# Linear attention on one core: the first half of Q is loaded by GpSimd with a cast instead of by SP in f32

## The chip, the core and the metric

The kernel runs on one core of one Trainium2 chip. The metric is the device time of one execution in microseconds (us). The median of three runs of the kernel before is 126.54 us (126.53 to 126.78).

## The reference

```python
def setup_inputs():
    batch, heads, seq, dim = 8, 12, 512, 64      # Q, K, V: f32, [8, 12, 512, 64] each
...
    Q_feat = np.maximum(0, Q) + 1
    K_feat = np.maximum(0, K) + 1
    KV = np.einsum('bhkd,bhkv->bhdv', K_feat, V)
    K_sum = np.sum(K_feat, axis=2)
    numerator = np.einsum('bhqd,bhdv->bhqv', Q_feat, KV)
    denominator = np.einsum('bhqd,bhd->bhq', Q_feat, K_sum)
    return (numerator / (denominator[:, :, :, None] + 1e-10)).astype(np.float32)
```

There are 96 heads of 512 rows by 64. Three inputs of 12.58 MB each are read and one output of 12.58 MB is written, all f32 in DRAM.

## The kernel before

The 96 heads are worked on in twelve groups of eight heads (`NG` is 12), and two groups share one input buffer and one output buffer. K, V and Q are loaded into SBUF as bf16: the DMA that GpSimd issues reads f32 from DRAM and casts on its way (`load`, `load_q`). Only the first half of the first Q buffer is different: SP issues a DMA of f32 into a tile of its own, `q_first` (L93), since the DMAs that SP issues here move data as it is. The other half of that buffer, `u[:, 1]` of `q_raw`, is loaded by GpSimd with the cast (L98).

For each group VectorE makes the features of K and Q (`feature`, L146: add 1, then max with 1), VectorE and ScalarE lay V out in blocks (`v_blocks`, L162 and L164), TensorE multiplies K's features with V (`keys_values`, L180) and transposes Q's features (L201), TensorE makes the output (L214), and VectorE divides (`norms`, L231 and L232). GpSimd issues the stores of the first ten groups (L135); SP issues the last three store DMAs (L138 and L141).

The order of all instructions is written out by hand under `tc.manual_schedule()`: each engine runs its instructions in the order of the program text and waits only for the data that it needs. So the order of the lines at L257 to L273 is the order in which GpSimd issues the first loads and does its memsets. It is:

```python
        nc.gpsimd.memset(zero, 0.0)
        q_first = load_first_q()
        load("k", (0,))
        load("v", (0,))
        load_rest_q(q_first)
        load("k", (1,))
        load("v", (1,))
```

After these GpSimd builds `identity` for the transposes and clears the sixteen parts of `kva_all` (L271), and then it issues the loads of the next pair (`load_pair(1)`). `zero` is a [128, 1] tile of f32 zeros. ScalarE copies it, broadcast, into parts of `v_all` (L250), and VectorE clears the rest of `v_all` (L249). The input pool has two buffers of each kind, so the load of a later pair waits until VectorE and ScalarE have read the buffer that it overwrites.

Of the kernel before, what the change touches and what calls it, by code (L numbers as in the profile page):

```python
# [8 lines left out]
FP32 = mybir.dt.float32  # L9
BF16 = mybir.dt.bfloat16  # L10
# [9 lines left out]
def kernel(  # L20
# [19 lines left out]
    nc = tc.nc  # L40

    B, H, S, D = Q.shape
    P = 128
    C = 8
    C2 = 2 * C
    C4 = 4 * C
# [7 lines left out]
    def view(t, c):  # L54
        return t.flatten_outer_dims().rearrange("(n p c) d -> p n c d", p=P, c=c)

    q_eights = view(Q, C4)
# [2 lines left out]
    o_dram = view(out, C)  # L60

    const = ctx.enter_context(tc.tile_pool(name="const", bufs=1))
    head_pool = ctx.enter_context(tc.tile_pool(name="head_pool", bufs=1))
    in_pool = ctx.enter_context(tc.tile_pool(name="in_pool", bufs=IN_BUFS))
    kf_pool = ctx.enter_context(tc.tile_pool(name="kf_pool", bufs=2))
    qf_pool = ctx.enter_context(tc.tile_pool(name="qf_pool", bufs=3))
# [11 lines left out]
    zero = const.tile([P, 1], FP32, name="zero")  # L78
# [4 lines left out]
    raw = {}  # L83
    bufs = {}
# [3 lines left out]
    outs = {}  # L88
    cells_of = {}

    def load_first_q():
        t = head_pool.tile([P, C4, D], FP32, name="q_first")
        nc.sync.dma_start(out=t, in_=q_eights[:, 0])  # L93
        return t

    def load_rest_q(t):
        u = in_pool.tile([P, 2, C4, D], BF16, name="q_raw")
        nc.gpsimd.dma_start(out=u[:, 1], in_=q_eights[:, 1])  # L98
        for e in range(2):
            raw["q", e] = [  # L100
                x.rearrange("p (r c) d -> p r c d", c=C)[:, :, 4 * e : 4 * e + 4]
                for x in (t, u[:, 1])
            ]

    def load(x, groups):
        s = groups[0] // 2
        if groups[0] % 2 == 0 or (x, s) not in bufs:
            bufs[x, s] = in_pool.tile([P, 4, C2, D], BF16, name=f"{x}_raw")
        if len(groups) == 2:
            ms = slice(0, 4)  # L110
            of = slice(4 * s, 4 * s + 4)
        else:
            ms = slice(groups[0] % 2, 4, 2)
            of = slice(4 * s + groups[0] % 2, 4 * s + 4, 2)
        nc.gpsimd.dma_start(out=bufs[x, s][:, ms], in_=drams[x][:, of])  # L115
        for g in groups:
            raw[x, g] = bufs[x, s][:, g % 2 : 4 : 2]
# [8 lines left out]
    def load_pair(s):  # L126
        load("k", (2 * s, 2 * s + 1))
        load("v", (2 * s, 2 * s + 1))
        load_q(s)

    def store(g):
        s = g // 2
        o_to = o_dram[:, 2 * NP * s : 2 * NP * s + 2 * NP]
        if g < NG - 2:
            nc.gpsimd.dma_start(out=o_to[:, g % 2 : 2 * NP : 2], in_=outs[s][:, g % 2 : 2 * NP : 2])  # L135
            return
        if g == NG - 2:
            nc.sync.dma_start(out=o_to[:, 0 : 2 * NP : 2], in_=outs[s][:, 0 : 2 * NP : 2])  # L138
            return
        for h in range(2):  # L140
            nc.sync.dma_start(  # L141
                out=o_to[:, 2 * h + g % 2 : 2 * NP : NP], in_=outs[s][:, 2 * h + g % 2 : 2 * NP : NP]
            )
# [6 lines left out]
    def k_features(g):  # L150
        k_raw = raw.pop(("k", g))
        kf = kf_pool.tile([P, C2, 2, D], BF16, name="kf")
        for n in range(2):
            feature(kf[:, :, n], k_raw[:, n])
        kfs[g] = kf

    def v_blocks(g):
        v_raw = raw.pop(("v", g))
        for b in range(4):
            ps = slice(32 * b, 32 * b + 32)  # L160
            if b == 3:
                nc.scalar.copy(out=v_all[ps, g % 2, :, :, b * D : b * D + D], in_=v_raw[ps])  # L162
            else:
                nc.vector.tensor_copy(  # L164
                    out=v_all[ps, g % 2, :, :, b * D : b * D + D], in_=v_raw[ps]
                )

    def q_features(g):
        q_raw = raw.pop(("q", g))
        qf = qf_pool.tile([P, R, C // 2, 2, D], BF16, name="qf")  # L170
        for n in range(2):
            feature(qf[:, :, :, n], q_raw[n])
        qfs[g] = qf

    def keys_values(g):
        kf = kfs.pop(g)
        kva_ps = psum_kva.tile([P, 4 * D1], FP32, name="kva_ps")
        for c in range(C2):
            for n in range(2):
                nc.tensor.matmul(  # L180
                    kva_ps[64 * n : 64 * n + 64],
                    lhsT=kf[:, c, n, :],
                    rhs=v_all[:, g % 2, n, c, :],
                    start=(c == 0),
                    stop=(c == C2 - 1),
                )
        kva = kva_diag[g % NV]
        for n in range(2):
            ps = slice(64 * n, 64 * n + 64)
            nc.scalar.copy(out=kva[ps, :, n, 0:D], in_=kva_ps[ps, 0 : 4 * D].rearrange("p (b d) -> p b d", b=4))  # L190
            nc.scalar.copy(out=kva[ps, :, n, D], in_=kva_ps[ps, 4 * D : 4 * D1])  # L191

    def transposes(g):
        qf = qfs.pop(g)
        if g % 2 == 0:
            qts[g // 2] = mid_pool.tile([P, C, P, R], BF16, name="qt")
        for half in range(2):
            qt_ps = psum_qt.tile([P, 2, R, P], BF16, name="qt_ps")
            for c in range(2):
                for r in range(R):  # L200
                    nc.tensor.transpose(qt_ps[:, c, r], qf[:, r, 2 * half + c, :, :], identity)  # L201
            copy = nc.vector.tensor_copy if half and g == NG - 2 else nc.scalar.copy
            lo = g % 2 * 4 + 2 * half
            copy(out=qts[g // 2][:, lo : lo + 2], in_=qt_ps.rearrange("p c r q -> p c q r"))  # L204
# [36 lines left out]
    def output(g):  # L241
        for h in range(2):
            out_matmuls(g, h)
            norms(g, h)

    def clear(i):
        t = v_all[:, i].rearrange("p n c x -> p (n c x)").bitcast(FP32)
        w = t.shape[1] * 5 // 8
        nc.vector.memset(t[:, 0:w], 0.0)  # L249
        nc.scalar.copy(out=t[:, w:], in_=zero.to_broadcast([P, t.shape[1] - w]))  # L250
        nc.vector.tensor_copy(
            out=v_all[:, i, :, :, 4 * D : 4 * D1].rearrange("p n c j -> p (n c) j"),
            in_=ones[:, None, :].to_broadcast([P, 2 * C2, 4]),
        )

    with tc.manual_schedule():
        nc.gpsimd.memset(zero, 0.0)  # L257
        q_first = load_first_q()
        load("k", (0,))
        load("v", (0,))  # L260
        load_rest_q(q_first)
        load("k", (1,))
        load("v", (1,))
        nc.vector.memset(ones, 0.0)
        for b in range(4):
            nc.vector.memset(ones[32 * b : 32 * b + 32, b : b + 1], 1.0)
        clear(0)
        make_identity(nc, identity)
        for t in kva_diag:
            for b in range(4):  # L270
                nc.gpsimd.memset(t[:, b], 0.0)  # L271
        load_pair(1)
        clear(1)  # L273
        last = NG - 1
        for g in range(last - 1):
            if g % 2:
                transposes(g - 1)
            k_features(g)
            v_blocks(g)
            if g >= 2:  # L280
                output(g - 2)
            if g % 2:
                transposes(g)
            else:
                q_features(g)
                q_features(g + 1)
            keys_values(g)
            if g % 2 and g // 2 + 2 < NG // 2:
                load_pair(g // 2 + 2)
            if g >= LAG:  # L290
                store(g - LAG)
        k_features(last - 1)
        output(last - 3)
        out_matmuls(last - 2, 0)
        v_blocks(last - 1)
        k_features(last)
        v_blocks(last)
        keys_values(last - 1)
        store(last - 1 - LAG)
        q_features(last - 1)  # L300
        q_features(last)
        norms(last - 2, 0)
        transposes(last - 1)
        out_matmuls(last - 2, 1)
        norms(last - 2, 1)
        transposes(last)
        keys_values(last)
        output(last - 1)
        output(last)
        for g in range(last - LAG, NG):  # L310
            store(g)
# [30 lines left out]
```

## Time and profile before

| | us |
|---|---|
| median of three runs | 126.54 |
| the profiled execution | 126.47 |
| its span, first to last instruction | 124.7 |
| VectorE (DVE) busy | 90.1 |
| TensorE (PE) busy | 64.2 |
| ScalarE (ACT) busy | 59.6 |
| GpSimd (POOL) busy | 26.1 |

The profiled execution took 1.8 us more than its span; that part lies around the instructions. In the profile "DMA" is the mean busy share of the core's sixteen DMA engines and "GB/s" is what they moved, counted by the bytes written: a load with the cast reads two bytes from DRAM for each byte that it writes into SBUF. Queue q0 (software_dynamic) carries the DMAs that GpSimd issues; q1 (hardware_dynamic) carries those that SP issues. A line "POOL ... DMA_DIRECT2D" is the time in which GpSimd makes the descriptors of a DMA, not the time in which its data moves.

### The profile page before, as it was taken

Reading aid. Unit: us, or ns where it says so; the run is one execution under the profiler, and the core shown is the slowest. Engines: PE = TensorE matmul, PEld = TensorE weight load, DVE = VectorE, ACT = ScalarE, POOL = GpSimd, SP = SyncE. Lnnn points to the kernel's source line nnn. Section 1 sums busy time; section 2 is a strip of 40 time slices with the busy share of each in tenths; the row PEclk is TensorE's granted clock in tenths of the full one; section 3 lists DMA queues with packets and bytes.
Section 4 is the critical chain, followed back from the end, with each engine's and each line's share of the span. In section 5 each row is a group of like instructions: output and inputs, shape, how many; then the busy total and the mean of one; then the engine's idle time right before and its main releaser. Section 6 shows DMA issues by size and latency. Waiting matters only on the chain.

```text
span 124.7 us, 2349 instructions
## 1 busy us (share of the span) xinstructions
PE 64.2 (52%) x960; PEld 52.6 (42%) x960; DVE 90.1 (72%) x190; ACT 59.6 (48%) x86; POOL 26.1 (21%) x53
## 2 busy tenths in 40 slices
PE   0000874600596837939099690069394369874200
PEld 0000654600475826829088490058183158663000
DVE  4875735206999989998999950799958799969700
ACT  7505169806009981398803981603982283650000
POOL 6992020400001460207202070302020200020000
PEclk9999999995559996799855999657999855999655
DMA  3999999999999999999999999999999999999993
GB/s 89 320 212 216 206 211 212 212 215 218 206 212 212 220 213 206 212 215 217 230 406 327 210 212 219 212 342 395 230 202 215 219 247 417 419 417 415 406 409 135
DMA packets 11819, 32.13 MB, mean 258 GB/s; under 512 B 544, under 2 KB 544, under 8 KB 11680
## 3 DMA queue, kind: packets, MB, share of 16 engines
q0 software_dynamic: 10592, 28.84, 97.5%
q1 hardware_dynamic: 1216, 3.15, 6.7%
q8 instruction: 7, 0.11, 0.3%
q14 instruction: 4, 0.03, 0.1%
HBM read 37.75 MB, written 12.58 MB: 404 GB/s over the span
## 4 chain that ended last, share of the span: by engine, by line
DMA 51%; DVE 19%; PE 10%; ACT 7%; POOL 6%; issue 2%; DVEq 0%; ACTq 0%; POOLq 0%
DMA v_raw<-in_V_dram 51%; DVE o_sb L232 7%; PE kva_ps L180 7%; DVE v_all L164 7%; ACT qt L204 3%; ACT v_all L162 3%; POOL kva_all L271 2%; POOL k_raw L115 2%; DVE recip L231 2%; PE qt_ps L201 1%; PE o_ps L214 1%; POOL v_raw L115 1%; DVE qf L146 1%; DVE qt L204 1%; DVE kf L146 1%
## 5 line engine op out<-in xcount | busy, mean ns | idle before, releaser
L180 PE MATMUL kva_ps<-v_all,kf 128*64 128x260 bf16 x384 | 33.0, 343 | 16.8 <-DVE v_all L164 15.5
L214 PE MATMUL o_ps<-kva_all,qt 128*64 128x130 bf16 x384 | 19.7, 237 | 34.2 <-DVE recip L231 25.9
L164 DVE COPY v_all<-v_raw 32x2048 bf16<-32x2048 bf16 x36 | 26.1, 725 | 15.0 <-DMA v_raw<-in_V_dram 14.6
L180 PEld LDWEIGHTS <-kf 128*64 128x64 bf16 x384 | 26.6, 140 | 20.4 <-DVE v_all L164 15.9
L232 DVE TENSOR_TENSOR o_sb<-o_ps,recip 128x512 f32<-128x512 f32 x48 | 33.2, 692 | 1.6
L162 ACT COPY v_all<-v_raw 32x2048 bf16<-32x2048 bf16 x12 | 22.6, 1893 | 18.2 <-DMA v_raw<-in_V_dram 18.0
L214 PEld LDWEIGHTS <-qt 128*64 128x64 bf16 x384 | 13.7, 116 | 39.1 <-issue 23.2
L190 ACT CAST kva_all<-kva_ps 64x256 bf16<-64x256 f32 x24 | 8.9, 370 | 30.7 <-PE kva_ps L180 30.6
L204 ACT COPY qt<-qt_ps 128x1024 bf16<-128x1024 bf16 x23 | 22.2, 1015 | 2.2 <-PE qt_ps L201 1.7
L201 PE MATMUL qt_ps<-identity,qf 128*128 128x128 bf16 x192 | 14.8, 236 | 1.3 <-ACT qt L204 1.1
L135 POOL DMA_DIRECT2D out_dram<-o_sb x10 | 8.3, 830 | 32.1 <-DVE o_sb L232 27.3
L146 DVE TENSOR_SCALAR kf<-k_raw 128x1024 bf16<-128x1024 bf16 x24 | 9.5, 436 | 7.0 <-DMA k_raw<-in_K_dram 7.0
L201 PEld LDWEIGHTS <-qf 128*128 128x128 bf16 x192 | 12.6, 107 | 4.1 <-issue 1.8
L115 POOL DMA_DIRECT2D k_raw<-in_K_dram x7 | 5.4, 765 | 34.4 <-DVE kf L146 34.0
L231 DVE RECIPROCAL recip<-o_ps 128x8 f32<-128x8 f32 x48 | 9.6, 200 | 1.5 <-PE o_ps L214 1.2
L115 POOL DMA_DIRECT2D v_raw<-in_V_dram x7 | 5.4, 772 | 17.4 <-ACT v_all L162 17.4
L146 DVE TENSOR_SCALAR qf<-q_raw 128x1024 bf16<-128x1024 bf16 x22 | 8.2, 432 | 0.0
L249 DVE MEMSET v_all<- 128x2600 f32 x2 | 4.5, 2225 | 1.1 <-issue 1.1
L191 ACT CAST kva_all<-kva_ps 64x4 bf16<-64x4 f32 x24 | 4.1, 169 | 0.0
L121 POOL DMA_DIRECT2D q_raw<-in_Q_dram x5 | 3.5, 705 | 0.0
L250 ACT COPY v_all<-zero 128x1560 f32<-128x1560 f32 x2 | 2.9, 1488 | 0.0
L271 POOL MEMSET kva_all<- 128x130 bf16 x16 | 2.4, 196 | 0.0
(14 smaller groups left out, 6.6 us busy)
## 6 DMA issues: line engine op xcount, KB each, us to landing
out_dram<-o_sb POOLq DMA_DIRECT2D x10, 1024.0 KB, 25.2
k_raw<-in_K_dram POOLq DMA_DIRECT2D x5, 1024.0 KB, 21.7
v_raw<-in_V_dram POOLq DMA_DIRECT2D x5, 1024.0 KB, 21.8
q_raw<-in_Q_dram POOLq DMA_DIRECT2D x5, 1024.0 KB, 25.9
q_first<-in_Q_dram SPq DMA_DIRECT2D x1, 1024.0 KB, 4.9
k_raw<-in_K_dram POOLq DMA_DIRECT2D x2, 512.0 KB, 9.7
v_raw<-in_V_dram POOLq DMA_DIRECT2D x2, 512.0 KB, 11.4
out_dram<-o_sb SPq DMA_DIRECT2D x1, 1024.0 KB, 7.0
```

The costliest lines, as they stand in the source:

```text
L115: nc.gpsimd.dma_start(out=bufs[x, s][:, ms], in_=drams[x][:, of])
L135: nc.gpsimd.dma_start(out=o_to[:, g % 2 : 2 * NP : 2], in_=outs[s][:, g % 2 : 2 * NP : 2])
L146: nc.vector.tensor_scalar(out=dst, in0=src, scalar1=1.0, scalar2=1.0, op0=ALU.add, op1=ALU.max)
L162: nc.scalar.copy(out=v_all[ps, g % 2, :, :, b * D : b * D + D], in_=v_raw[ps])
L164: nc.vector.tensor_copy(out=v_all[ps, g % 2, :, :, b * D : b * D + D], in_=v_raw[ps])
L180: nc.tensor.matmul(kva_ps[64 * n : 64 * n + 64], lhsT=kf[:, c, n, :], rhs=v_all[:, g % 2, n, c, :], start=(c == 0), stop=(c == C2 - 1),)
L190: nc.scalar.copy(out=kva[ps, :, n, 0:D], in_=kva_ps[ps, 0 : 4 * D].rearrange("p (b d) -> p b d", b=4))
L201: nc.tensor.transpose(qt_ps[:, c, r], qf[:, r, 2 * half + c, :, :], identity)
L204: copy(out=qts[g // 2][:, lo : lo + 2], in_=qt_ps.rearrange("p c r q -> p c q r"))
L214: nc.tensor.matmul(ops[c // 4][64 * j : 64 * j + 64, c // 2 % 2, (c % 2) * W : (c % 2) * W + W], lhsT=qt[:, c, q : q + 16, :], rhs=kva[:, ...
L231: nc.vector.reciprocal(out=recip, in_=cells[:, :, :, :, D:D1])
L232: nc.vector.tensor_tensor(out=o_sb[:, 2 * h + g % 2 : 2 * NP : NP, 4 * i : 4 * i + 4].rearrange("p n (b c) d -> p b c n d", b=2), in0=cell ...
```

## The change

The f32 load from SP and its tile `q_first` are gone. Both halves of the first Q buffer are loaded by GpSimd with the cast into the two halves of one `q_raw` tile, which existed before with one half unused. The load of the first half is GpSimd's first instruction after the program's preamble, ahead of the loads of K and V; the second half stays at its place. The memset of `zero` moves from GpSimd to VectorE, as VectorE's first instruction. SP has no work left until the stores at the end. VectorE's features of that half read bf16 instead of f32.

```diff
-    head_pool = ctx.enter_context(tc.tile_pool(name="head_pool", bufs=1))
...
-    def load_first_q():
-        t = head_pool.tile([P, C4, D], FP32, name="q_first")
-        nc.sync.dma_start(out=t, in_=q_eights[:, 0])
-        return t
-
-    def load_rest_q(t):
-        u = in_pool.tile([P, 2, C4, D], BF16, name="q_raw")
-        nc.gpsimd.dma_start(out=u[:, 1], in_=q_eights[:, 1])
+    def load_half_q(n):
+        if n == 0:
+            bufs["q", 0] = in_pool.tile([P, 2, C4, D], BF16, name="q_raw")
+        t = bufs["q", 0]
+        nc.gpsimd.dma_start(out=t[:, n], in_=q_eights[:, n])
+        rows = t.rearrange("p n (r c) d -> p n r c d", c=C)
         for e in range(2):
-            raw["q", e] = [
-                x.rearrange("p (r c) d -> p r c d", c=C)[:, :, 4 * e : 4 * e + 4]
-                for x in (t, u[:, 1])
-            ]
+            raw["q", e] = [rows[:, m, :, 4 * e : 4 * e + 4] for m in range(2)]
...
     with tc.manual_schedule():
-        nc.gpsimd.memset(zero, 0.0)
-        q_first = load_first_q()
+        nc.vector.memset(zero, 0.0)
+        load_half_q(0)
         load("k", (0,))
         load("v", (0,))
-        load_rest_q(q_first)
+        load_half_q(1)
         load("k", (1,))
         load("v", (1,))
```

## The prediction

> **What bounds the kernel now.** I read the page's slices and queues first, then the busy time by stretches, and then the timeline of the start and of the end.
>
> ```profile
> DMA  3999999999999999999999999999999999999993
> GB/s 89 320 212 216 206 211 212 212 215 218 206 212 212 220 213 206 212 215 217 230 406 327 210 212 219 212 342 395 230 202 215 219 247 417 419 417 415 406 409 135
> q0 software_dynamic: 10592, 28.84, 97.5%
> HBM read 37.75 MB, written 12.58 MB: 404 GB/s over the span
> ```
>
> The DMA engines are full in 38 of the 40 slices; only the first and the last are not. VectorE, the busiest compute engine, is busy for 90 of 124.7 us. Plain transfers run at 406 to 419 GB/s. Loads with the cast show about 212 GB/s written, which is 424 GB/s read from DRAM. So both kinds cost the same per byte of DRAM: 37.75 + 12.58 = 50.33 MB at 0.42 MB per us is 120 us. The start shows from when:
>
> ```profile
> 0.00:1.50 1.50, 0.00 (x0) 0.00 (x0) 0.30 (x5) 0.76 (x1) 0.51 (x6) 1.00 0.00 0
> 1.50:2.00 0.50, 0.00 (x0) 0.00 (x0) 0.13 (x1) 0.50 (x1) 0.50 (x1) 1.00 1.13 131
> 2.00:2.50 0.50, 0.00 (x0) 0.00 (x0) 0.50 (x1) 0.49 (x2) 0.50 (x2) 1.00 0.00 0
> 2.50:3.00 0.50, 0.00 (x0) 0.00 (x0) 0.50 (x1) 0.50 (x1) 0.50 (x2) 1.00 0.68 279
> 3.00:3.50 0.50, 0.00 (x0) 0.00 (x0) 0.50 (x1) 0.50 (x2) 0.50 (x2) 1.00 0.97 410
> 4.50:5.00 0.50, 0.00 (x0) 0.00 (x0) 0.11 (x1) 0.41 (x1) 0.50 (x2) 1.00 1.17 483
> 5.00:5.50 0.50, 0.00 (x0) 0.00 (x0) 0.50 (x1) 0.00 (x0) 0.43 (x3) 1.00 1.06 168
> 116.00:121.00 5.00, 0.48 (x8) 0.24 (x8) 1.55 (x4) 0.00 (x0) 0.00 (x0) 0.52 1.03 408
> ```
>
> The last two columns are the busy share of the DMA engines and GB/s. Added up from 1.5 to 5.0 us (two more stretches of 459 and 344 GB/s lie between), these rows moved 1053 KB: all of `q_first` (1049 KB) and next to nothing else. At 5.0 us the rate falls to that of cast loads with no idle time between. At full rate 1.049 MB takes 1.049/0.424 = 2.47 us, so `q_first` did as much as a stream that starts at full rate at 5.0 - 2.5 = 2.5 us; call this the effective start. From 2.5 us to about 123.4 us, where the last rates end, the engines have no gap, and those 120.9 us are what 50.33 MB need. The kernel is one DMA stream, and its end moves with its effective start.
>
> **The change part by part.**
>
> ```profile
> 0.74 0.10 POOL L257 MEMSET zero<- 128x1 f32 x1 [0.29 <-POOLq L326]
> 0.74 0.39 SPq L93 DMA_DIRECT2D q_first<-in_Q_dram  x1
> 1.29 0.84 POOL L115 DMA_DIRECT2D k_raw<-in_K_dram  x1 [0.46 <-issue]
> 2.13 0.73 POOL L115 DMA_DIRECT2D v_raw<-in_V_dram  x1
> 2.85 0.57 POOL L98 DMA_DIRECT2D q_raw<-in_Q_dram  x1
> ```
>
> *Removed: SP's load.* SP needs 0.39 us from 0.74 us, so it is done at 1.13 us, and the stream's effective start is 1.4 us after that. Meanwhile GpSimd makes its first descriptors. This is the cover that goes: in the kernel before nobody sees how long GpSimd's first DMA takes to bring data, for `q_first` fills the engines until 5.0 us.
>
> *Added: GpSimd's load as the first of the stream.* Three terms give the new effective start.
>
> (a) When the instruction begins. The other engines begin at 0.74 us, and so does GpSimd with its memset. Its first DMA then waits 0.46 us for nothing that the profile shows. Ends: 0.74 us if the gap belonged to the memset, 1.29 us if nothing changes. A later row tells which is nearer: in the chain of waits GpSimd's DMA on L115 begins 0.29 us after ScalarE's copy that released it, where other engines follow in 0.02 to 0.06 us. So a DMA on GpSimd has a lead time of its own, and I take the gap as staying and the memset as leaving: 0.74 + 0.46 = 1.20 us.
>
> (b) How long it makes descriptors. The same shape (half a Q buffer) took 0.57 us; GpSimd's first DMA took 0.84 us, 0.11 more than the same shape next (0.73 us). I take 0.57 + 0.11 = 0.68 us; ends 0.57 and 0.84 us.
>
> (c) From there to the effective start. The nearest row is SP's own 1.4 us. No row shows GpSimd's, so both ends stay. Low: SP's data first shows in the stretch from 1.5 us, and its sixteen engines then need until 3.0 us to be full; a GpSimd queue that is full at once would take about 0.6 us. High: `k_raw`'s descriptors end at 1.29 + 0.84 = 2.13 us and its data runs at full rate from 5.0 us, so 2.9 us is enough. I take 1.4 us.
>
> The sum: 1.20 + 0.68 + 1.4 = 3.28 us against 2.5 us, a loss of 0.75 us. Low end: 0.74 + 0.57 + 0.6 = 1.9 us, a gain of 0.6 us. High end: 1.29 + 0.84 + 2.9 = 5.0 us, a loss of 2.5 us.
>
> The Trainium skill, "DMA: Bandwidth & Descriptors", sections "SWDGE vs HWDGE vs iDMA" and "Latency and other measured facts", says that descriptors made by GpSimd are slower to set up, with a first byte after about 1 us against about 0.6 us for SP's. SP's row here, 1.13 us to the stretch from 1.5 us, fits the second figure, and no row shows the first. By that page term (c) would be 0.4 us longer, an estimate, and the loss 1.15 us.
>
> *The transfer itself.* It reads the same 1.049 MB of DRAM. 213 GB/s written by casts is 426 read, the plain load had 410 to 459; the difference is nothing. Half the bytes are written into SBUF, but DRAM bytes set the rate in every slice.
>
> *GpSimd's later work.* One DMA more (0.57 to 0.84 us) and one memset less (0.10 us): all that follows comes about 0.5 us later: the five half loads, `identity`, the sixteen memsets of `kva_all` until 7.8 us, `load_pair(1)` from 7.75 us. The five half loads hold the queue until 5.0 + 5 x 2.47 = 17.3 us, so the pair's loads have 8 us of cover. `identity` is first used at 16.6 us, `kva_all` at 16.8 us. No cost; without this cover it would be 0.5 us.
>
> *SP's queue.* Its stores, L138 and L141, become its first DMAs:
>
> ```profile
> 114.28 0.39 SPq L138 DMA_DIRECT2D out_dram<-o_sb  x1
> 115.96 2.05 SPq L141 DMA_DIRECT2D out_dram<-o_sb  x2
> ```
>
> The rate stays at 408 GB/s from 116 to 121 us, so GpSimd's stores in the queue cover the 1.4 us start that SP showed at L93. Stores and loads shift together, so this stays. No cost; uncovered it would be up to 1.4 us.
>
> *VectorE.* The memset of `zero` costs it 0.06 to 0.10 us at 0.8 us. Behind it are queued `ones` and the big memsets, which end with L251 at 7.84 us; `k_raw` lands at 8.3 us, later now. ScalarE's L250 waits for `zero`, but its table load lasts from 0.74 to 2.02 us. No cost; uncovered 0.1 us. The two features of `q_first` fall from 0.69 to 0.42 us each, 0.5 us in all near 13 us; the next V block waits for its load anyway at 18.2 us. No gain.
>
> *What is late next.* All compute follows the loads and moves with them. The last SP store is issued by 118.0 us and the data runs until 123.4 us; about 2 MB of stores, 4.9 us, remain at 118.4 us, so the compute keeps its margin.
>
> The profiled 126.47 us is 0.07 under the median of 126.54. So 126.47 + 0.75 + 0.07 = 127.3 us.
>
> **The rivals.** What a measurement of this kernel can tell from no change is 0.2%, or 0.25 us.
>
> *A long cold start on GpSimd* (slower still). Term (c) is between 2.1 and 2.9 us: making the rings ready and fetching descriptors and the first data takes longer than SP's way. For it: nothing before 5.0 us shows GpSimd's data. Against it: at 5.0 us its data takes over at full rate without the ramp that SP's had from 1.5 to 3.0 us, so it was ready some time before. Loss 1.4 to 2.5 us: 127.9 to 129.0 us, most likely 128.2.
>
> *A faster start* (faster). GpSimd begins at 0.74 us because the memset and its gap are gone, takes 0.57 us, and all sixteen engines start together, without the share of 0.00 and 0.68 at 2.0 to 3.0 us. It decides when (a) + (b) + (c) is under 2.25 us; at its end, 1.9 us, the time is 125.9 us, in the middle 126.1. For it: the ramp of SP's load is poor. Against it: the lead time of 0.29 us and the slower descriptors.
>
> *No difference that shows.* The terms come out between 2.25 and 2.75 us: for example 1.02 (0.74 + 0.28) + 0.57 + 1.0 = 2.6 us. Time 126.5 us.
>
> That the change does not do what it says can be left out: the instructions show GpSimd's first DMA as the half of Q, and SP without a load.
>
> **How the numbers follow.** My forecast, a loss of 0.25 to 1.4 us (126.8 to 127.9), has 0.56; the long cold start 0.22; no difference 0.12; the faster start 0.10. So faster is 0.10, the same 0.12, slower 0.56 + 0.22 = 0.78. The range of 8 in 10 goes from 126.4, which leaves out most of the faster start, to 128.5, which leaves out the upper third of the cold start.
>
> **What would show it.** In the profile after: the first GpSimd DMA begins near 1.2 us and lasts about 0.7; the DMA share is zero past 2.0 us and full from about 3.3 us; the slices between stay full; the first K features on L146 begin about 0.75 us after 8.31 us; the span grows by just that shift. A first full rate by 2.5 us, an empty slice later on, or a shift at the start that is not found at the end would prove it wrong.

## The result: 0.5% slower, and the profile after

The changed kernel takes 127.40 us (median of 21 runs; 126.61 for the kernel before in the same comparison). The ratio is 1.0053, with a 95% interval of 1.0036 to 1.0070. The forecast was 127.3 us, slower.

The page of the kernel after: slices and queues.

```profile
DMA  1999999999999999999999999999999999999993
GB/s 13 180 209 219 206 210 210 212 214 215 207 214 211 217 218 204 213 212 216 217 390 356 209 211 217 214 313 411 243 211 213 216 249 407 420 413 417 409 408 148
q0 software_dynamic: 10736, 29.36, 99.3%
q1 hardware_dynamic: 1072, 2.10, 4.3%
HBM read 37.75 MB, written 12.58 MB: 402 GB/s over the span
```

The DMA digits are the same from the second slice to the last. Only the first slice differs, 1 where it was 3. `q_first` is gone from q1: its 2.10 MB are the three stores of SP.

The timeline of the start, kernel after:

```profile
0.81 0.06 DVE L251 MEMSET zero<- 128x1 f32 x1 [0.81 <-PEq L320]
1.27 0.69 POOL L94 DMA_DIRECT2D q_raw<-in_Q_dram  x1 [0.82 <-POOLq L320]
1.96 0.72 POOL L109 DMA_DIRECT2D k_raw<-in_K_dram  x1
8.96 1.04 DVE L140 TENSOR_SCALAR kf<-k_raw 128x1024 bf16<-128x1024 bf16 x2 [0.61 <-DMA k_raw<-in_K_dram]
```

GpSimd begins its first DMA at 1.27 us, although nothing is ahead of it any more, and is done at 1.96 us; SP was done at 1.13 us. The first K features begin at 8.96 us instead of 8.31. Now the busy time by stretches, again with DMA share and GB/s in the last two columns:

```profile
2.00:2.50 0.50, 0.00 (x0) 0.00 (x0) 0.50 (x1) 0.49 (x2) 0.50 (x1) 1.00 0.00 0
2.50:3.00 0.50, 0.00 (x0) 0.00 (x0) 0.50 (x1) 0.50 (x1) 0.50 (x2) 1.00 0.92 66
3.00:3.50 0.50, 0.00 (x0) 0.00 (x0) 0.50 (x1) 0.50 (x2) 0.50 (x2) 1.00 0.55 82
3.50:4.00 0.50, 0.00 (x0) 0.00 (x0) 0.50 (x1) 0.50 (x2) 0.50 (x2) 1.00 0.89 180
4.00:4.50 0.50, 0.00 (x0) 0.00 (x0) 0.39 (x2) 0.50 (x1) 0.50 (x1) 1.00 0.97 197
116.00:121.00 5.00, 1.01 (x16) 0.52 (x12) 2.11 (x5) 0.00 (x0) 0.00 (x0) 0.50 1.03 409
121.00:123.50 2.50, 0.00 (x0) 0.00 (x0) 0.00 (x0) 0.00 (x0) 0.00 (x0) 0.50 0.88 342
```

A share above 1.00 comes about because this view counts a packet, with all its time, in the stretch in which it begins.

No data before 2.5 us, a ramp, and the full rate, about 204 GB/s written (408 read), only from about 4 us. Added up as in the prediction, 2.5 to 5.5 us (two more stretches, of 221 and 188 GB/s, lie behind 4.5 us) hold 467 KB of the half buffer's 524; the rest takes 0.28 us more, so the half is in at 5.78 us and the effective start is 5.78 - 2.47 = 3.31 us, against 2.5 us. The end shows the same shift: 342 GB/s between 121.0 and 123.5 us, where the kernel before had 261:

```profile
121.00:123.50 2.50, 0.00 (x0) 0.00 (x0) 0.00 (x0) 0.00 (x0) 0.00 (x0) 0.50 0.68 261
```

This profiled execution took 127.04 us, the quickest of its runs, so its span grew by only 0.6 us.

### The profile page after: what moved, and what is told of

It is laid out like the page before. It is cut to its first block, busy times and chain, and to the rows that moved or that the text cites. A ratio compares the mean times of both kernels' runs of the same rounds, so it can differ in the third digit from the quotient of the medians.

```text
span 125.3 us, 2348 instructions
## 1 busy us (share of the span) xinstructions
PE 63.1 (50%) x960; PEld 51.7 (41%) x960; DVE 90.0 (72%) x191; ACT 59.6 (48%) x86; POOL 26.6 (21%) x53
## 4 chain that ended last, share of the span: by engine, by line
DMA 47%; DVE 23%; PE 11%; ACT 9%; issue 3%; POOL 1%; POOLq 0%
DMA v_raw<-in_V_dram 47%; DVE v_all L158 8%; PE kva_ps L174 8%; DVE o_sb L226 8%; ACT v_all L156 5%; ACT qt L198 3%; PE qt_ps L195 2%; DVE qf L140 2%; DVE recip L225 2%; DVE kf L140 1%; DVE qt L198 1%; ACT kva_all L184 1%; POOL k_raw L109 1%; POOL q_raw L94 1%; PE o_ps L208 1%
## 5 line engine op out<-in xcount | busy, mean ns | idle before, releaser
L174 PE MATMUL kva_ps<-v_all,kf 128*64 128x260 bf16 x384 | 31.6, 333 | 17.6 <-DVE v_all L158 15.9
L174 PEld LDWEIGHTS <-kf 128*64 128x64 bf16 x384 | 25.9, 136 | 21.2 <-DVE v_all L158 16.7
L140 DVE TENSOR_SCALAR qf<-q_raw 128x1024 bf16<-128x1024 bf16 x24 | 8.8, 430 | 0.0
```

The lines of the kernel that those rows point to most:

```text
L140: nc.vector.tensor_scalar(out=dst, in0=src, scalar1=1.0, scalar2=1.0, op0=ALU.add, op1=ALU.max)
L174: nc.tensor.matmul(kva_ps[64 * n : 64 * n + 64], lhsT=kf[:, c, n, :], rhs=v_all[:, g % 2, n, c, :], start=(c == 0), stop=(c == C2 - 1),)
```

## The experiments

Theory S is that of the prediction: one full DMA stream, whose end moves with its effective start. Its rivals: M, the moved memset or the new order of the start costs the time; C, the cast makes the first load worse; A, slack behind the start absorbs a late start, and the loss comes from elsewhere. Times are medians, with that of the kernel before in the same comparison.

**The memset alone** (e1): `nc.gpsimd.memset(zero, 0.0)` becomes `nc.vector.memset(zero, 0.0)` in the kernel before.

> SP's f32 load of the first half of Q stays; only the memset of zero moves to VectorE. Theory S (one full DMA stream whose end moves with its effective start): SP's load still starts the stream near 2.5 us and covers GpSimd's start until 5.0 us, so the time is that of the kernel before, 126.6 us (within 0.25 us), although GpSimd's first DMA may begin earlier. If the 0.46 us gap ahead of GpSimd's first DMA belonged to the memset, that DMA begins at 0.74 us; if it is the DMA's own lead, at 1.2 to 1.3 us. Rival M (the memset on VectorE or the other order of the start costs the time): 127.3 us or more.

126.80 us beside 126.91; ratio 0.9995 (0.9969 to 1.0022). M falls. The timeline of this kernel:

```profile
0.74 0.38 SPq L93 DMA_DIRECT2D q_first<-in_Q_dram  x1
1.27 0.84 POOL L115 DMA_DIRECT2D k_raw<-in_K_dram  x1 [0.83 <-POOLq L326]
8.22 0.84 DVE L146 TENSOR_SCALAR kf<-k_raw 128x1024 bf16<-128x1024 bf16 x2 [0.38 <-DMA k_raw<-in_K_dram]
```

The DMA begins at 1.27 us without the memset and at 1.29 with it: the gap is a lead of GpSimd's first DMA, about 0.53 us after SP could begin.

**The load alone** (e2): in the kernel after, the memset goes back to GpSimd, ahead of the load.

> GpSimd loads the first half of Q with the cast, but the memset of zero stays on GpSimd ahead of it. Theory S with a lead time of GpSimd's DMA that covers the memset: the DMA begins at 1.27 to 1.3 us as in the changed kernel, and the time is that of the changed kernel, 127.3 us, ratio 1.005. If the memset were in the way: the DMA begins 0.1 us or more later and the time is 127.4 to 127.9 us.

127.89 us beside 126.91; ratio 1.0073 (1.0047 to 1.0098). The DMA begins at 1.30 us and the first K features at 9.15. The whole loss comes with the load. The interval overlaps that of the changed kernel, which a second comparison (e8, below) put at 1.0074, so the memset's place makes no difference that shows.

**No cast** (e3): GpSimd loads `q_first` as f32.

```diff
-        nc.sync.dma_start(out=t, in_=q_eights[:, 0])
+        nc.gpsimd.dma_start(out=t, in_=q_eights[:, 0])
...
-        nc.gpsimd.memset(zero, 0.0)
+        nc.vector.memset(zero, 0.0)
```

> GpSimd issues the first half of Q as plain f32 into the f32 tile, without the cast; the memset is on VectorE as in the changed kernel. Theory S (what costs is that GpSimd starts the stream, whatever it moves): the first DMA begins near 1.27 us, lasts about 0.7 us, the stream's effective start is near 3.2 us, and the time is 127.2 to 127.5 us, ratio 1.005. Rival C (the cast, with its smaller packets, ramps worse than plain f32): the time falls back toward 126.6 us.

127.47 us beside 126.91; ratio 1.0036 (1.0009 to 1.0063). Slower than before, as S has it, and below the 1.005 that was expected. The DMA begins at 1.28 us, lasts 0.69, and the first K features begin at 9.02 us, within the 8.96 and 9.05 of the two profiles of the changed kernel. So the start is as late without the cast. C falls as the main cause. In the same comparison e3 is 0.42 us below e2, which has the cast, with intervals that overlap; so these runs leave room for a share of the cast up to about that size, and do not show one.

**A later start** (e4): in the kernel after, the loop with the sixteen memsets of `kva_all` goes ahead of `load_half_q(0)`.

> The changed kernel with the sixteen memsets of kva_all (2.4 us on GpSimd) ahead of GpSimd's first load instead of behind the six half loads. Theory S: the stream starts later by 2.0 to 2.4 us (the memsets may run under the DMA's lead time of about 0.5 us) and the end moves by the same amount: first K features near 11.2 us, time 129.3 to 129.8 us, ratio 1.020 to 1.025. Rival A (slack somewhere behind the start absorbs a late start, so that the change's loss comes from another place): under 128.3 us.

129.14 us beside 126.91; ratio 1.0166 (1.0130 to 1.0203). The expected 129.3 was missed, since the delay was smaller than thought. The timeline of this kernel:

```profile
0.74 2.34 POOL L254 MEMSET kva_all<- 128x130 bf16 x16 [0.29 <-POOLq L320]
3.02 0.69 POOL L94 DMA_DIRECT2D q_raw<-in_Q_dram  x1
10.99 0.43 DVE L140 TENSOR_SCALAR kf<-k_raw 128x1024 bf16<-128x1024 bf16 x1 [3.55 <-DMA k_raw<-in_K_dram]
```

The lead of 0.53 us passes under the memsets, and the load begins 3.02 - 1.27 = 1.75 us later. Medians of the two kernels differ by 129.14 - 127.40 = 1.74 us, the ratios by 0.0113 or 1.4 us, from two comparisons. Within one comparison there is e2, whose load begins 1.72 us before that of e4: its median lies 129.14 - 127.89 = 1.25 us lower. So 1.2 to 1.7 us of the delay reach the end, and A, which needed a time under 128.3 us, falls as the explanation; whether up to half a microsecond of so long a delay is absorbed, these runs do not tell.

**The same delay behind SP's load** (e5): the same loop ahead of `load("k", (0,))` in the kernel before.

> The kernel before (SP loads q_first) with the sixteen memsets of kva_all ahead of GpSimd's first load, so that GpSimd's first DMA starts near 3.0 us as it did with the same memsets in the changed kernel. Theory S with a cover: GpSimd's data is ready about 1.3 us after its descriptors, 3.0 + 0.84 + 1.3 = 5.2 us, where q_first ends at 5.0 to 5.3 us; the same delay that cost the changed kernel about 1.7 us costs 0 to 0.3 us here. Rival (SP's load does not cover GpSimd's start; each delay of GpSimd's queue costs its length): 1.4 to 1.8 us, about 128.4 us.

127.01 us beside 126.65; ratio 1.0017 (0.9994 to 1.0040), that is 0.2 us.

```profile
0.74 0.38 SPq L93 DMA_DIRECT2D q_first<-in_Q_dram  x1
3.07 0.84 POOL L115 DMA_DIRECT2D k_raw<-in_K_dram  x1
8.71 0.91 DVE L146 TENSOR_SCALAR kf<-k_raw 128x1024 bf16<-128x1024 bf16 x2 [1.30 <-DMA k_raw<-in_K_dram]
```

GpSimd's first DMA is 1.78 us later than before and the first K features only 0.40 us. SP's load had covered GpSimd's start, with some 1.4 us to spare. That cover is what the change takes away.

**Could the start be earlier?** Four more kernels split `q_first`; e8 is the changed kernel once more, beside two of them.

e6 splits by partitions over two queues:

```diff
-        nc.sync.dma_start(out=t, in_=q_eights[:, 0])
+        nc.sync.dma_start(out=t[0:64], in_=q_eights[0:64, 0])
+        nc.scalar.dma_start(out=t[64:128], in_=q_eights[64:128, 0])
```

> The kernel before with q_first loaded by two queues at once: SP takes partitions 0 to 63, ScalarE's queue partitions 64 to 127. If SP's descriptor time (0.39 us) and the late start of half of the DMA engines (the rate of 0 between 2.0 and 2.4 us) come from one queue serving the engines one after the other, the effective start moves from 2.5 us toward 1.9 to 2.2 us, and by theory S the time falls by 0.3 to 0.6 us, to about 126.1 to 126.3 us. If the ramp is the DMA engines' own cold latency, the time stays within 0.2 us of before. ScalarE's table load starts later by the issue, which its later idle time covers.

128.14 us beside 126.65; ratio 1.0112 (1.0079 to 1.0144): the expectation failed both ways. The stretches of this kernel:

```profile
3.00:5.00 2.00, 0.00 (x0) 0.00 (x0) 1.41 (x3) 2.00 (x2) 2.00 (x4) 1.00 1.07 246
3.50:4.00 0.50, 0.00 (x0) 0.00 (x0) 0.50 (x1) 0.50 (x1) 0.50 (x1) 1.00 1.30 262
4.00:4.50 0.50, 0.00 (x0) 0.00 (x0) 0.29 (x2) 0.50 (x2) 0.50 (x2) 1.00 0.87 180
4.50:5.00 0.50, 0.00 (x0) 0.00 (x0) 0.11 (x1) 0.50 (x1) 0.50 (x2) 1.00 0.80 197
```

The DMA engines count as busy, yet from 3.0 to 5.0 us f32 moves at 246 GB/s (180 to 344 in single half microseconds), where the kernel before moved 424. By the trace's packets SP's half moves from 2.07 to 4.63 us and ScalarE's from 4.17 to 7.02: the two halves go almost wholly one after the other. The first K features begin at 9.88 us.

e7 has two DMAs on SP, `t[:, 0:16]` and then `t[:, 16:32]`.

> The kernel before with q_first loaded by SP in two DMAs of half the columns each. If what holds the start back is the size of the first DMA's descriptors, the first data comes earlier and the effective start is 0.1 to 0.3 us earlier: 126.2 to 126.4 us. If it is a fixed latency, nothing changes, or up to 0.3 us is lost to the smaller packets: 126.5 to 126.8 us.

126.97 us beside 126.65; ratio 1.0021 (0.9999 to 1.0043). No gain; the time lies a little above the range of the second case. SP makes descriptors for 0.87 us and the first K features begin at 8.88 us. With all partitions in each DMA, the rate comes up to that of the kernel before, if later:

```profile
4.50:5.00 0.50, 0.00 (x0) 0.00 (x0) 0.12 (x1) 0.42 (x1) 0.50 (x2) 1.00 1.03 414
```

> The changed kernel as it is, beside the others on one chip. Theory S: first K features near 8.96 us, the time 0.6 to 0.8 us over the kernel before, ratio 1.005 to 1.006.

127.59 us beside 126.65; ratio 1.0074 (1.0047 to 1.0101), first K features at 9.05 us: somewhat above the expected ratio, with an interval that overlaps the first comparison's.

What slowed e6, the half of the partitions or the second queue, is told apart by two more. e9 gives SP `t[:, 0:16]` and ScalarE's queue `t[:, 16:32]`:

> The kernel before with q_first split by columns: SP loads the first sixteen rows of every partition, ScalarE's queue the other sixteen. The split by partitions over the same two queues cost about 1.4 us: its packets took 0.52 to 0.67 us instead of 0.31, and the stream's effective start was 1.6 us later. If that came from each DMA writing only 64 of the 128 partitions, the packets here are fast again and the time is 126.5 to 127.1 us. If it came from a second hardware queue beside SP's and GpSimd's, it stays near 128 us.

126.60 us beside 126.62; ratio 0.9981 (0.9950 to 1.0013). Its stretches:

```profile
2.50:3.00 0.50, 0.00 (x0) 0.00 (x0) 0.50 (x1) 0.50 (x1) 0.50 (x2) 1.00 0.86 279
3.50:4.00 0.50, 0.00 (x0) 0.00 (x0) 0.50 (x1) 0.50 (x2) 0.50 (x1) 1.00 1.06 426
4.00:4.50 0.50, 0.00 (x0) 0.00 (x0) 0.29 (x2) 0.50 (x1) 0.50 (x2) 1.00 1.07 410
3.00:5.00 2.00, 0.00 (x0) 0.00 (x0) 1.41 (x3) 2.00 (x2) 2.00 (x4) 1.00 1.02 399
```

e10 has SP alone issue partitions 0 to 63 and then 64 to 127:

> The kernel before with q_first loaded by SP alone in two DMAs, partitions 0 to 63 and then 64 to 127. If a DMA that writes half of the partitions runs at half the rate, the loss of the split by partitions over two queues, 1.2 to 1.6 us, is found here too: 127.8 to 128.3 us. If the second queue was the reason, the time is that of the two column DMAs on SP, 126.8 to 127.1 us.

128.24 us beside 126.62; ratio 1.0110 (1.0049 to 1.0172). Its stretches:

```profile
3.00:5.00 2.00, 0.00 (x0) 0.00 (x0) 1.41 (x3) 1.91 (x2) 2.00 (x4) 1.00 1.03 218
4.50:5.00 0.50, 0.00 (x0) 0.00 (x0) 0.11 (x1) 0.41 (x1) 0.50 (x2) 1.00 0.96 217
```

From 3.0 to 5.0 us two queues with all partitions move 399 GB/s (e9), and one queue with half of the partitions at a time moves 218. e7, which has the same queue and the same number of DMAs as e10 but all partitions in each, moved 314 GB/s in that stretch, with 414 at its end, and has a ratio of 1.0021 against 1.0110. So the half is the reason, and not the second queue. Each of these DMAs also reads only one half of the region in DRAM; whether the writing or the reading halves the rate, these runs do not tell apart. None of the four splits beats the kernel before, so no better version came out.

Profiled executions, by when the first K features begin:

| kernel | first K features, us | that execution, us |
|---|---|---|
| e1, memset alone | 8.22 | 126.64 |
| before | 8.31 | 126.47 |
| e9, split by columns | 8.46 | 126.59 |
| e5, delay behind SP's load | 8.71 | 127.46 |
| e7, two DMAs on SP | 8.88 | 127.17 |
| after, and again | 8.96, 9.05 | 127.04, 127.40 |
| e3, no cast | 9.02 | 127.48 |
| e2, load alone | 9.15 | 127.88 |
| e6, split by partitions | 9.88 | 127.67 |
| e10, the same on SP | 10.17 | 128.22 |
| e4, later start | 10.99 | 129.23 |

From the first row to the last the features shift by 2.77 us and the time by 2.59. In between, single executions scatter by up to some 0.6 us around that line.

## Why the prediction was right

*One stream, end to end.* Shown by e4 (some 1.75 us of delay, of which 1.2 to 1.7 us reach the end) and by the table. The compute's margin at the end held: 409 GB/s from 116 to 121 us.

*Term (a)*, taken as 1.20 us, measured 1.27. The step was wrong in a detail: I let the memset's 0.10 us leave and the gap stay behind it. The lead runs beside whatever is ahead of the DMA, one memset (e2: 1.30 us) or sixteen (e4: none left), so removing the memset freed 0.02 us. That also ends the rival of a faster start, which needed 0.74 us here.

*Term (b)*, taken as 0.68 us, measured 0.69.

*Term (c)*, taken from SP's row as 1.4 us, measured 3.31 - 1.96 = 1.35 us. This was the term with the widest ends, 0.6 and 2.9. Neither the immediate start of all engines nor the long cold start came: GpSimd's queue ramps like SP's. No row of the kernel before could say so: that SP's row would fit GpSimd was a guess that came true. The sum was 3.28 us and came out as 3.31.

The loss therefore lies ahead of the queue: GpSimd's descriptors are done 1.96 - 1.13 = 0.83 us after SP's, 0.53 by the lead and 0.30 by the longer instruction. That sum, and the shift of the effective start by 0.8 us, agree with the medians' 0.79 us (0.94 in the second comparison).

*The page that I weighed.* The Trainium skill, "DMA: Bandwidth & Descriptors", section "Latency and other measured facts", gives a first byte after about 0.6 us from SP and about 1 us from GpSimd and puts the difference down to emission. In stretches of 0.2 us SP's first data (kernel before) shows from 1.6 us and GpSimd's (kernel after) from 2.6:

```profile
1.60:1.80 0.20, 0.00 (x0) 0.00 (x0) 0.00 (x0) 0.20 (x1) 0.20 (x1) 1.00 1.77 205
2.60:2.80 0.20, 0.00 (x0) 0.00 (x0) 0.20 (x1) 0.20 (x1) 0.20 (x2) 1.00 2.29 164
```

From the begin of the instruction that is 0.9 and 1.3 us, each about 0.3 us above the page's figure, but with the page's difference of 0.4; from its end it is 0.5 and 0.6. I had added the page's 0.4 us to term (c), behind the 0.68 us of term (b), where it was counted already; by the rows alone the sum is right, by the page it would have been 0.4 us too long.

*What cost nothing, as said.* The memset on VectorE (e1). GpSimd's later work: in the kernel after `load_pair(1)` is issued from 8.24 us, 0.49 us later, and no slice shows it. SP's stores as its first DMAs. VectorE's four Q features take 1.46 us from 13.60 us, where they took 1.97, and the next V block waits for its load at 18.87 us: no gain.

*What was a little off.* I expected a full rate from about 3.3 us. The rate climbs from 2.5 to 4.0 us, and 3.3 us is its effective start. The first K features, forecast 0.75 us later, came 0.65 us later in the first profile and 0.74 in the second (e8). I also took the 0.00 between 2.0 and 2.5 us of the kernel before for a gap in the ramp of SP's load. The stretch before it, 131 GB/s for 0.5 us, holds eight packets of 8 KB, and its share of 1.13 gives each of them about 1.1 us: they were still under way while no new one began. And the upper end of the long cold start was added up with the high ends of all three terms; with (a) and (b) as I took them, a term (c) of 2.9 us makes the loss 2.25 us, not 2.5.

## What to carry to other kernels

Where the DMA engines are full from end to end, as here, look first at the moment from which they are full: compare first loads by when their descriptors are done and add the ramp of each queue, which here was the same for both. The first load on the queue that starts soonest paid twice here: it started the stream, and it hid the start of the slower queue behind it, with about 1.4 us to spare. A smaller or faster operation that such a change brings along, such as the bf16 features, was worth nothing here.

## What the runs showed that was not expected

A DMA that writes 64 of the 128 partitions runs at little more than half the rate: 246 GB/s (e6) and 218 (e10) from 3.0 to 5.0 us, against 399 with all partitions (e9), while the DMA engines count as busy. And GpSimd's first DMA does not begin before 1.27 us, whether one memset or nothing is ahead of it, while SP's and ScalarE's DMAs began at 0.74 us; what fills the 0.53 us the profile does not show, and it stays open.
